# A batch normalisation that streams through two DMA rings: Tile's dependencies in place of hand-made semaphores, and an early 128-byte write by each DMA engine

## The chip, the cores and the metric

One core of a Trainium2 chip. The time is device microseconds of that core. Before: 2484.66 us (median of 3 runs, 2484.28 to 2487.45). With a single core there is no second die to compare; every run listed here except the single one of `touch_allrows` (state unknown) is classed fast.

## The reference

```python
x = np.random.randn(32, 256, 128, 128).astype(np.float32)      # 537 MB
# gamma, beta, running_mean, running_var: 256 floats each
return gamma * (x - mean) / np.sqrt(var + 1e-5) + beta         # per channel
```

Per channel it is one multiply and one add: `scale = gamma / sqrt(var + eps)`, `shift = beta - mean * scale`. All the rest is moving 537 MB in and 537 MB out.

## The kernel before

The input is 64 tiles of 128 rows x 16,384 floats (8.4 MB, 64 KB a row). Three buffers hold tiles. Loads are issued from SyncE and stores from ScalarE: two rings of descriptors on the same 16 DMA engines. Of each tile VectorE does columns 0 to 14,335 in two instructions (2560 columns first), ScalarE the last 2048 (7168 of the last tile). Both rings are paced on purpose: load i waits for the first vector part of tile i-1, and the scalar part of tile i waits until store i-1 has landed.

```python
for i in range(1, NT):                                     # SyncE
    s, turn = i % NBUF, i // NBUF
    if turn:
        nc.sync.wait_ge(stored[s], 16 * turn)              # the buffer is free
    inst = nc.sync.dma_start(out=bufs[s][:], in_=xr[i]).then_inc(loaded[s], 16)
    if turn:
        inst._wait_ge(vdone, 2 * (i - 1) + 1)              # first vector part of tile i-1
# ...
vector_part(0, 0, HW // 2)._wait_ge(early, 16)             # VectorE
vector_part(0, HW // 2, VCOLS)._wait_ge(*landed(0))
for i in range(1, NT):
    vector_part(i, 0, STEP)._wait_ge(*landed(i))           # STEP = 2560
    vector_part(i, STEP, VLAST if i == last else VCOLS)    # VCOLS = 14336
for i in range(last):                                      # ScalarE
    nc.scalar.wait_ge(vdone, 2 * (i + 1))
    inst = scalar_part(i, VCOLS)
    if i:
        inst._wait_ge(stored[(i - 1) % NBUF], 16 * ((i - 1) // NBUF + 1))
    store(i)
```

Of the kernel before, what the change touches and what calls it, by code (L numbers as in the profile page):

```python
# [8 lines left out]
NBUF = 3  # L9


STEP = 2560
VCOLS = 14336
VLAST = 9216


@with_exitstack
def kernel(
    ctx: ExitStack,
    tc: tile.TileContext,  # L20
    x: bass.AP,
    gamma: bass.AP,
    beta: bass.AP,
    running_mean: bass.AP,
    running_var: bass.AP,
    out: bass.AP,
):
    nc = tc.nc
    eps = 1e-5
    f32 = mybir.dt.float32  # L30

    N, C, H, W = x.shape
    P = nc.NUM_PARTITIONS
    assert C % P == 0
    NCB = C // P
    HW = H * W
    NT = N * NCB
    B = 32
    NQ = P // B
    NE = 16  # L40
    NPAR = 4

    xr = x.rearrange("n (cb p) h w -> (n cb) p (h w)", p=P)
    outr = out.rearrange("n (cb p) h w -> (n cb) p (h w)", p=P)

    params = ctx.enter_context(tc.tile_pool(name="params", bufs=1))
    data = ctx.enter_context(tc.tile_pool(name="data", bufs=1))
    bufs = [data.tile([P, HW], f32, name=f"t{s}", tag=f"t{s}") for s in range(NBUF)]
    rows = params.tile([B, NPAR * C], f32, name="rows", tag="rows")
    turned = params.tile([B, NPAR * C], f32, name="turned", tag="turned")  # L50
    par = params.tile([P, NPAR, NCB], f32, name="par", tag="par")
    eps_t = params.tile([P, 1], f32, name="eps_t", tag="eps")
    std_t = params.tile([P, NCB], f32, name="std_t", tag="std")
    rstd_t = params.tile([P, NCB], f32, name="rstd_t", tag="rstd")
    scale_t = params.tile([P, NCB], f32, name="scale_t", tag="scale")
    ms_t = params.tile([P, NCB], f32, name="ms_t", tag="ms")
    shift_t = params.tile([P, NCB], f32, name="shift_t", tag="shift")



    loaded = [tc.alloc_semaphore(f"loaded{s}") for s in range(NBUF)]
    stored = [tc.alloc_semaphore(f"stored{s}") for s in range(NBUF)]
    early = tc.alloc_semaphore("early")
    vdone = tc.alloc_semaphore("vdone")
    adone = tc.alloc_semaphore("adone")
    fetched = tc.alloc_semaphore("fetched")
    vec = tc.alloc_semaphore("vec")
    act = tc.alloc_semaphore("act")

    with tc.tile_critical():  # L70
        count = [0]

        def step(inst, sem=None, value=None):

            if sem is not None:
                inst._wait_ge(sem, value)
            elif count[0]:
                inst._wait_ge(vec, count[0])
            inst.then_inc(vec, 1)
            count[0] += 1  # L80
            return count[0]

        left, right = slice(0, HW // 2), slice(HW // 2, HW)
        last = NT - 1



        nc.sync.dma_start(out=bufs[0][:, left], in_=xr[0][:, left]).then_inc(early, 16)
        zeroed = step(nc.vector.memset(rows[:], 0.0))  # L89
        for r, ap in enumerate((running_var, gamma, beta, running_mean)):  # L90
            inst = nc.sync.dma_start(out=rows[0:NE, r * C : (r + 1) * C], in_=ap.partition_broadcast(NE))  # L91
            if r == 0:
                inst._wait_ge(vec, zeroed)
            inst.then_inc(fetched, 16)
        nc.sync.dma_start(out=bufs[0][:, right], in_=xr[0][:, right]).then_inc(loaded[0], 16)  # L95
        for i in range(1, NT):
            s, turn = i % NBUF, i // NBUF


            if turn:  # L100
                nc.sync.wait_ge(stored[s], 16 * turn)
            inst = nc.sync.dma_start(out=bufs[s][:], in_=xr[i]).then_inc(loaded[s], 16)
            if turn:
                inst._wait_ge(vdone, 2 * (i - 1) + 1)


        step(nc.vector.memset(eps_t[:], eps))  # L107
        step(nc.vector.transpose(out=turned[:], in_=rows[:]), fetched, 16 * NPAR)  # L108

        blocks = turned.rearrange("p (rc q b) -> p rc q b", q=NQ, b=B)  # L110
        flat = par.rearrange("p r cb -> p (r cb)")
        for q in range(NQ):
            placed = step(nc.vector.tensor_copy(out=flat[q * B : (q + 1) * B], in_=blocks[:, :, q, 0]))  # L113
        var_t, gamma_t, beta_t, mean_t = (par[:, r] for r in range(NPAR))
        nc.scalar.activation(  # L115
            out=std_t[:],
            in_=var_t,
            func=mybir.ActivationFunctionType.Sqrt,
            bias=eps_t[:],
            scale=1.0,  # L120
        )._wait_ge(vec, placed).then_inc(act, 1)
        step(nc.vector.reciprocal(out=rstd_t[:], in_=std_t[:]), act, 1)  # L122
        step(nc.vector.tensor_mul(out=scale_t[:], in0=gamma_t, in1=rstd_t[:]))  # L123
        step(nc.vector.tensor_mul(out=ms_t[:], in0=mean_t, in1=scale_t[:]))  # L124
        ready = step(nc.vector.tensor_sub(out=shift_t[:], in0=beta_t, in1=ms_t[:]))  # L125
        nc.vector.wait_ge(vec, ready)

        def vector_part(i, first, end):
            t, cb = bufs[i % NBUF], i % NCB
            return nc.vector.tensor_scalar(  # L130
                out=t[:, first:end],
                in0=t[:, first:end],
                scalar1=scale_t[:, cb : cb + 1],
                scalar2=shift_t[:, cb : cb + 1],
                op0=mybir.AluOpType.mult,
                op1=mybir.AluOpType.add,
            ).then_inc(vdone, 1)

        def scalar_part(i, first):
            t, cb = bufs[i % NBUF], i % NCB  # L140
            return nc.scalar.activation(  # L141
                out=t[:, first:],
                in_=t[:, first:],
                func=mybir.ActivationFunctionType.Identity,
                bias=shift_t[:, cb : cb + 1],
                scale=scale_t[:, cb : cb + 1],
            ).then_inc(adone, 1)

        def landed(i):
            return loaded[i % NBUF], 16 * (i // NBUF + 1)  # L150

        def store(i):
            s = i % NBUF
            nc.scalar.dma_start(out=outr[i], in_=bufs[s][:])._wait_ge(adone, i + 1).then_inc(stored[s], 16)

        vector_part(0, 0, HW // 2)._wait_ge(early, 16)
        vector_part(0, HW // 2, VCOLS)._wait_ge(*landed(0))
        for i in range(1, NT):
            vector_part(i, 0, STEP)._wait_ge(*landed(i))
            vector_part(i, STEP, VLAST if i == last else VCOLS)  # L160
        for i in range(last):
            nc.scalar.wait_ge(vdone, 2 * (i + 1))
            inst = scalar_part(i, VCOLS)
            if i:
                inst._wait_ge(stored[(i - 1) % NBUF], 16 * ((i - 1) // NBUF + 1))
            store(i)
        scalar_part(last, VLAST)._wait_ge(*landed(last))
        nc.scalar.wait_ge(vdone, 2 * NT)
        store(last)

        for s in range(NBUF):
            nc.sync.wait_ge(stored[s], 16 * ((NT - s + NBUF - 1) // NBUF))


# [28 lines left out]
```

## Time and profile before

| | before |
|---|---|
| time, median | 2484.66 us |
| span of the profiled run | 2483.3 us |
| moved | 1073.85 MB, mean 432 GB/s |
| VectorE / ScalarE busy | 20% / 6% |
| a 64 KB DMA packet (median) | 2.418 us |
| store issue after load issue, each turn | 24.6 us |

How the page itself is read stands in the prediction. One measure is used all through and comes from the trace's records of single DMA packets: by how much the 64 KB packets exceed 2.418 us, summed and divided by 16 engines. The part of it at the first store's arrival is called the stretch at the first store, the rest other lengthening.

### The profile page before, as it was taken

Reading aid. Unit: us, or ns where it says so; the run is one execution under the profiler, and the core shown is the slowest. Engines: PE = TensorE matmul, PEld = TensorE weight load, DVE = VectorE, ACT = ScalarE, POOL = GpSimd, SP = SyncE. Lnnn points to the kernel's source line nnn. Section 1 sums busy time; section 2 is a strip of 40 time slices with the busy share of each in tenths; the row PEclk is TensorE's granted clock in tenths of the full one; section 3 lists DMA queues with packets and bytes.
Section 4 is the critical chain, followed back from the end, with each engine's and each line's share of the span. In section 5 each row is a group of like instructions: output and inputs, shape, how many; then the busy total and the mean of one; then the engine's idle time right before and its main releaser. Section 6 shows DMA issues by size and latency. Waiting matters only on the chain.

```text
span 2483.3 us, 516 instructions
## 1 busy us (share of the span) xinstructions
DVE 508.8 (20%) x139; ACT 139.8 (6%) x66; POOL 0.2 (0%) x4
## 2 busy tenths in 40 slices
DVE  3122121221212212122121221212212122121220
ACT  0000000000000000000000000000000000000001
POOL 0000000000000000000000000000000000000000
DMA  9999999999999999999999999999999999999999
GB/s 415 430 439 434 428 436 436 435 433 430 432 433 438 430 432 433 435 424 437 437 428 436 438 436 429 437 435 430 436 437 436 430 437 435 429 437 435 433 433 408
DMA packets 18708, 1073.85 MB, mean 432 GB/s; under 512 B 2128, under 2 KB 2192, under 8 KB 2192
## 3 DMA queue, kind: packets, MB, share of 16 engines
q1 hardware_dynamic: 9488, 536.94, 50.1%
q10 hardware_dynamic: 9216, 536.88, 49.9%
q14 instruction: 4, 0.03, 0.0%
HBM read 536.94 MB, written 536.87 MB: 432 GB/s over the span
## 4 chain that ended last, share of the span: by engine, by line
DMA 93%; DVE 4%; another core or an unknown queue 1%; ACT 0%; issue 0%; SPq 0%; DVEq 0%
DMA t<-in_x_dram 93%; DVE t L130 4%; ACT t L141 0%; SPq L91 0%; DVE rows L89 0%; SPq L95 0%; DVE eps_t L107 0%; DVEq L198 0%; SPq L70 0%
## 5 line engine op out<-in xcount | busy, mean ns | idle before, releaser
L130 DVE TENSOR_SCALAR t<-t,scale_t,shift_t 128x11776 f32<-128x11776 f32 (+2 forms) x128 | 505.3, 3989 | 1930.4 <-DMA t<-in_x_dram 1930.2
L141 ACT ACTIVATE t<-t,shift_t,scale_t 128x2048 f32<-128x2048 f32 x64 | 138.2, 2159 | 2299.3 <-DMA out_dram<-t 2276.6
L108 DVE STREAM_TRANSPOSE turned<-rows 32x1024 f32<-32x1024 f32 x1 | 1.2, 1233 | 12.5 <-DMA rows<-in_running_mean_dram 12.5
L115 ACT ACT_TABLE_LOAD x1 | 1.3, 1283 | 0.9 <-SPq L70 0.9
L89 DVE MEMSET rows<- 32x1024 f32 x1 | 0.9, 912 | 1.2 <-SPq L70 1.2
L115 ACT ACTIVATE std_t<-par,eps_t 128x2 f32<-128x2 f32 x1 | 0.3, 296 | 14.7 <-DVE par L113 14.7
L113 DVE COPY par<-turned 32x8 f32<-32x8 f32 x4 | 0.6, 161 | 0.1
L122 DVE RECIPROCAL rstd_t<-std_t 128x2 f32<-128x2 f32 x1 | 0.2, 166 | 0.4 <-ACT std_t L115 0.4
L125 DVE TENSOR_TENSOR shift_t<-par,ms_t 128x2 f32<-128x2 f32 x1 | 0.2, 161 | 0.0
L124 DVE TENSOR_TENSOR ms_t<-par,scale_t 128x2 f32<-128x2 f32 x1 | 0.2, 161 | 0.0
L123 DVE TENSOR_TENSOR scale_t<-par,rstd_t 128x2 f32<-128x2 f32 x1 | 0.2, 160 | 0.0
L187 POOL MEMSET const-bfloat16-1.0<- 128x1 bf16 x1 | 0.1, 101 | 0.0
L187 POOL MEMSET const-uint8-127<- 128x1 uint8 x1 | 0.1, 101 | 0.0
L187 POOL MEMSET const-float32-0.0<- 128x1 f32 x1 | 0.1, 98 | 0.2 <-issue 0.2
L187 POOL MEMSET const-float32-1.0<- 128x1 f32 x1 | 0.1, 98 | 0.0
L107 DVE MEMSET eps_t<- 128x1 f32 x1 | 0.1, 59 | 0.1
## 6 DMA issues: line engine op xcount, KB each, us to landing
t<-in_x_dram SPq DMA_DIRECT2D x2, 4096.0 KB, 16.5
out_dram<-t ACTq DMA_DIRECT2D x64, 36.5
t<-in_x_dram SPq DMA_DIRECT2D x63, 37.0
rows<-in_running_var_dram SPq DMA_DIRECT2D x1, 16.0 KB, 11.3
rows<-in_gamma_dram SPq DMA_DIRECT2D x1, 16.0 KB, 11.1
rows<-in_beta_dram SPq DMA_DIRECT2D x1, 16.0 KB, 10.9
rows<-in_running_mean_dram SPq DMA_DIRECT2D x1, 16.0 KB, 11.3
```

The lines of the kernel that those rows point to most:

```text
L89: zeroed = step(nc.vector.memset(rows[:], 0.0))
L107: step(nc.vector.memset(eps_t[:], eps))
L108: step(nc.vector.transpose(out=turned[:], in_=rows[:]), fetched, 16 * NPAR)
L113: placed = step(nc.vector.tensor_copy(out=flat[q * B : (q + 1) * B], in_=blocks[:, :, q, 0]))
L115: nc.scalar.activation(out=std_t[:], in_=var_t, func=mybir.ActivationFunctionType.Sqrt, bias=eps_t[:], scale=1.0,)._wait_ge(vec, placed).t ...
L122: step(nc.vector.reciprocal(out=rstd_t[:], in_=std_t[:]), act, 1)
L123: step(nc.vector.tensor_mul(out=scale_t[:], in0=gamma_t, in1=rstd_t[:]))
L124: step(nc.vector.tensor_mul(out=ms_t[:], in0=mean_t, in1=scale_t[:]))
L125: ready = step(nc.vector.tensor_sub(out=shift_t[:], in0=beta_t, in1=ms_t[:]))
L130: return nc.vector.tensor_scalar(out=t[:, first:end], in0=t[:, first:end], scalar1=scale_t[:, cb : cb + 1], scalar2=shift_t[:, cb : cb + 1 ...
L141: return nc.scalar.activation(out=t[:, first:], in_=t[:, first:], func=mybir.ActivationFunctionType.Identity, bias=shift_t[:, cb : cb + 1] ...
L187: nc = _bacc.Bacc("TRN2", target_bir_lowering=False, num_devices=1)
```

## The change

The hand-made semaphores go, and Tile derives the waits from the buffers; two dependencies added by hand keep the pace. New is a touch: before its first store, each DMA engine writes 128 bytes into a row of the first output tile (they are overwritten later), so that whatever a first write costs is paid early.

```diff
-    bufs = [data.tile([P, HW], f32, name=f"t{s}", tag=f"t{s}") for s in range(NBUF)]
-    loaded = [tc.alloc_semaphore(f"loaded{s}") for s in range(NBUF)]
-    # ... seven more kinds of semaphores, and every wait on them
+    data = ctx.enter_context(tc.tile_pool(name="data", bufs=NBUF))
+    ctx.enter_context(tc.manual_schedule())
+    def after(inst, other):
+        info = mybir.DependencyInfo(mybir.DependencyClass.Sync, mybir.DependencyReason.DATA)
+        tc.add_manual_dep(inst.ins, other.ins.name, info, reason="pace of the rings")
 # ...
+    blank = params.tile([P, B], f32, tag="blank")
+    nc.vector.memset(blank[:], 0.0)
+    touch = nc.scalar.dma_start(out=outr[0][0 :: P // NE, 0:B], in_=blank[0 :: P // NE])
 # ...
+        mine = scalar_part(i, VLAST if i == last else VCOLS)
+        if 0 < i < last:
+            after(mine, stores[i - 1])
+        if i == 0:
+            after(mine, touch)
+        stores[i] = nc.scalar.dma_start(out=outr[i], in_=tiles[i][:])
+        if 2 <= i and i + 1 < NT:
+            after(load(i + 1), firsts[i])
```

More of the change, by code (lines that the diff above doesn't have):

```diff
@@ L46 @@
     params = ctx.enter_context(tc.tile_pool(name="params", bufs=1))
-    data = ctx.enter_context(tc.tile_pool(name="data", bufs=1))
-    bufs = [data.tile([P, HW], f32, name=f"t{s}", tag=f"t{s}") for s in range(NBUF)]
-    rows = params.tile([B, NPAR * C], f32, name="rows", tag="rows")
-    turned = params.tile([B, NPAR * C], f32, name="turned", tag="turned")
-    par = params.tile([P, NPAR, NCB], f32, name="par", tag="par")
-    eps_t = params.tile([P, 1], f32, name="eps_t", tag="eps")
-    std_t = params.tile([P, NCB], f32, name="std_t", tag="std")
@@ L54 @@
-    rstd_t = params.tile([P, NCB], f32, name="rstd_t", tag="rstd")
-    scale_t = params.tile([P, NCB], f32, name="scale_t", tag="scale")
-    ms_t = params.tile([P, NCB], f32, name="ms_t", tag="ms")
-    shift_t = params.tile([P, NCB], f32, name="shift_t", tag="shift")
-    loaded = [tc.alloc_semaphore(f"loaded{s}") for s in range(NBUF)]
-    stored = [tc.alloc_semaphore(f"stored{s}") for s in range(NBUF)]
-    early = tc.alloc_semaphore("early")
-    vdone = tc.alloc_semaphore("vdone")
-    adone = tc.alloc_semaphore("adone")
@@ L66 @@
-    fetched = tc.alloc_semaphore("fetched")
-    vec = tc.alloc_semaphore("vec")
-    act = tc.alloc_semaphore("act")
-    with tc.tile_critical():
-        count = [0]
-        def step(inst, sem=None, value=None):
-            if sem is not None:
-                inst._wait_ge(sem, value)
-            elif count[0]:
-                inst._wait_ge(vec, count[0])
-            inst.then_inc(vec, 1)
-            count[0] += 1
-            return count[0]
-        left, right = slice(0, HW // 2), slice(HW // 2, HW)
-        last = NT - 1
-        nc.sync.dma_start(out=bufs[0][:, left], in_=xr[0][:, left]).then_inc(early, 16)
-        zeroed = step(nc.vector.memset(rows[:], 0.0))
-        for r, ap in enumerate((running_var, gamma, beta, running_mean)):
-            inst = nc.sync.dma_start(out=rows[0:NE, r * C : (r + 1) * C], in_=ap.partition_broadcast(NE))
-            if r == 0:
-                inst._wait_ge(vec, zeroed)
-            inst.then_inc(fetched, 16)
-        nc.sync.dma_start(out=bufs[0][:, right], in_=xr[0][:, right]).then_inc(loaded[0], 16)
-        for i in range(1, NT):
-            s, turn = i % NBUF, i // NBUF
-            if turn:
-                nc.sync.wait_ge(stored[s], 16 * turn)
-            inst = nc.sync.dma_start(out=bufs[s][:], in_=xr[i]).then_inc(loaded[s], 16)
-            if turn:
-                inst._wait_ge(vdone, 2 * (i - 1) + 1)
-        step(nc.vector.memset(eps_t[:], eps))
-        step(nc.vector.transpose(out=turned[:], in_=rows[:]), fetched, 16 * NPAR)
-        blocks = turned.rearrange("p (rc q b) -> p rc q b", q=NQ, b=B)
-        flat = par.rearrange("p r cb -> p (r cb)")
-        for q in range(NQ):
-            placed = step(nc.vector.tensor_copy(out=flat[q * B : (q + 1) * B], in_=blocks[:, :, q, 0]))
-        var_t, gamma_t, beta_t, mean_t = (par[:, r] for r in range(NPAR))
-        nc.scalar.activation(
-            out=std_t[:],
-            in_=var_t,
-            func=mybir.ActivationFunctionType.Sqrt,
-            bias=eps_t[:],
-            scale=1.0,
-        )._wait_ge(vec, placed).then_inc(act, 1)
-        step(nc.vector.reciprocal(out=rstd_t[:], in_=std_t[:]), act, 1)
-        step(nc.vector.tensor_mul(out=scale_t[:], in0=gamma_t, in1=rstd_t[:]))
-        step(nc.vector.tensor_mul(out=ms_t[:], in0=mean_t, in1=scale_t[:]))
-        ready = step(nc.vector.tensor_sub(out=shift_t[:], in0=beta_t, in1=ms_t[:]))
-        nc.vector.wait_ge(vec, ready)
-        def vector_part(i, first, end):
-            t, cb = bufs[i % NBUF], i % NCB
-            return nc.vector.tensor_scalar(
-                out=t[:, first:end],
-                in0=t[:, first:end],
-                scalar1=scale_t[:, cb : cb + 1],
-                scalar2=shift_t[:, cb : cb + 1],
-                op0=mybir.AluOpType.mult,
-                op1=mybir.AluOpType.add,
-            ).then_inc(vdone, 1)
-        def scalar_part(i, first):
-            t, cb = bufs[i % NBUF], i % NCB
-            return nc.scalar.activation(
-                out=t[:, first:],
-                in_=t[:, first:],
-                func=mybir.ActivationFunctionType.Identity,
-                bias=shift_t[:, cb : cb + 1],
-                scale=scale_t[:, cb : cb + 1],
-            ).then_inc(adone, 1)
-        def landed(i):
-            return loaded[i % NBUF], 16 * (i // NBUF + 1)
-        def store(i):
-            s = i % NBUF
-            nc.scalar.dma_start(out=outr[i], in_=bufs[s][:])._wait_ge(adone, i + 1).then_inc(stored[s], 16)
-        vector_part(0, 0, HW // 2)._wait_ge(early, 16)
-        vector_part(0, HW // 2, VCOLS)._wait_ge(*landed(0))
-        for i in range(1, NT):
-            vector_part(i, 0, STEP)._wait_ge(*landed(i))
-            vector_part(i, STEP, VLAST if i == last else VCOLS)
-        for i in range(last):
-            nc.scalar.wait_ge(vdone, 2 * (i + 1))
-            inst = scalar_part(i, VCOLS)
-            if i:
-                inst._wait_ge(stored[(i - 1) % NBUF], 16 * ((i - 1) // NBUF + 1))
-            store(i)
-        scalar_part(last, VLAST)._wait_ge(*landed(last))
-        nc.scalar.wait_ge(vdone, 2 * NT)
-        store(last)
-        for s in range(NBUF):
-            nc.sync.wait_ge(stored[s], 16 * ((NT - s + NBUF - 1) // NBUF))
@@ new lines, with load @@
+    data = ctx.enter_context(tc.tile_pool(name="data", bufs=NBUF))
[3 more added lines that the diff above has]
+        tc.add_manual_dep(inst.ins, other.ins.name, info, reason="pace of the rings")
+    last = NT - 1
+    left, right = slice(0, HW // 2), slice(HW // 2, HW)
+    tiles, firsts, stores = {}, {}, {}
+    def load(i):
+        t = data.tile([P, HW], f32, tag="t")
+        tiles[i] = t
+        return nc.sync.dma_start(out=t[:], in_=xr[i])
@@ new lines @@
+    t = data.tile([P, HW], f32, tag="t")
+    tiles[0] = t
+    nc.sync.dma_start(out=t[:, left], in_=xr[0][:, left])
+    rows = params.tile([B, NPAR * C], f32, tag="rows")
+    nc.vector.memset(rows[:], 0.0)
+    for r, ap in enumerate((running_var, gamma, beta, running_mean)):
+        nc.sync.dma_start(out=rows[0:NE, r * C : (r + 1) * C], in_=ap.partition_broadcast(NE))
+    nc.sync.dma_start(out=t[:, right], in_=xr[0][:, right])
+    load(1)
+    load(2)
+    blank = params.tile([P, B], f32, tag="blank")
@@ new lines @@
+    nc.vector.memset(blank[:], 0.0)
+    touch = nc.scalar.dma_start(out=outr[0][0 :: P // NE, 0:B], in_=blank[0 :: P // NE])
+    eps_t = params.tile([P, 1], f32, tag="eps")
+    nc.vector.memset(eps_t[:], eps)
+    turned = params.tile([B, NPAR * C], f32, tag="turned")
+    nc.vector.transpose(out=turned[:], in_=rows[:])
+    par = params.tile([P, NPAR, NCB], f32, tag="par")
+    blocks = turned.rearrange("p (rc q b) -> p rc q b", q=NQ, b=B)
+    flat = par.rearrange("p r cb -> p (r cb)")
+    for q in range(NQ):
+        nc.vector.tensor_copy(out=flat[q * B : (q + 1) * B], in_=blocks[:, :, q, 0])
@@ new lines @@
+    var_t, gamma_t, beta_t, mean_t = (par[:, r] for r in range(NPAR))
+    scale_t = params.tile([P, NCB], f32, tag="scale")
+    shift_t = params.tile([P, NCB], f32, tag="shift")
+    tmp_t = params.tile([P, NCB], f32, tag="tmp")
+    nc.scalar.activation(
+        out=tmp_t[:],
+        in_=var_t,
+        func=mybir.ActivationFunctionType.Sqrt,
+        bias=eps_t[:],
+        scale=1.0,
+    )
+    nc.vector.reciprocal(out=tmp_t[:], in_=tmp_t[:])
+    nc.vector.tensor_mul(out=scale_t[:], in0=gamma_t, in1=tmp_t[:])
@@ new lines, with vector_part, scalar_part @@
+    nc.vector.tensor_mul(out=tmp_t[:], in0=mean_t, in1=scale_t[:])
+    nc.vector.tensor_sub(out=shift_t[:], in0=beta_t, in1=tmp_t[:])
+    def vector_part(i, first, end):
+        t, cb = tiles[i], i % NCB
+        return nc.vector.tensor_scalar(
+            out=t[:, first:end],
+            in0=t[:, first:end],
+            scalar1=scale_t[:, cb : cb + 1],
+            scalar2=shift_t[:, cb : cb + 1],
+            op0=mybir.AluOpType.mult,
+            op1=mybir.AluOpType.add,
+        )
+    def scalar_part(i, first):
+        t, cb = tiles[i], i % NCB
+        return nc.scalar.activation(
+            out=t[:, first:],
+            in_=t[:, first:],
+            func=mybir.ActivationFunctionType.Identity,
+            bias=shift_t[:, cb : cb + 1],
+            scale=scale_t[:, cb : cb + 1],
+        )
@@ new lines @@
+    for i in range(NT):
+        if i == 0:
+            vector_part(0, 0, HW // 2)
+            vector_part(0, HW // 2, VCOLS)
+        else:
+            firsts[i] = vector_part(i, 0, STEP)
+            vector_part(i, STEP, VLAST if i == last else VCOLS)
+        mine = scalar_part(i, VLAST if i == last else VCOLS)
+        if 0 < i < last:
+            after(mine, stores[i - 1])
+        if i == 0:
+            after(mine, touch)
+        stores[i] = nc.scalar.dma_start(out=outr[i], in_=tiles[i][:])
+        if 2 <= i and i + 1 < NT:
+            after(load(i + 1), firsts[i])
```

## The prediction

> **What bounds the kernel now.** I read the page's head and its slices first, then its chain, then its groups of instructions, and last the order of time at both ends of the span.
>
> ```profile
> span 2483.3 us, 516 instructions
> DVE 508.8 (20%) x139; ACT 139.8 (6%) x66; POOL 0.2 (0%) x4
> ...
> DMA  9999999999999999999999999999999999999999
> ...
> GB/s 415 430 439 434 428 436 436 435 433 430 432 433 438 430 432 433 435 424 437 437 428 436 438 436 429 437 435 430 436 437 436 430 437 435 429 437 435 433 433 408
> ...
> DMA t<-in_x_dram 93%; DVE t L130 4%; ACT t L141 0%; SPq L91 0%; DVE rows L89 0%; SPq L95 0%; DVE eps_t L107 0%; DVEq L198 0%; SPq L70 0%
> ...
> L130 DVE TENSOR_SCALAR t<-t,scale_t,shift_t 128x11776 f32<-128x11776 f32 (+2 forms) x128 | 505.3, 3989 | 1930.4 <-DMA t<-in_x_dram 1930.2
> L141 ACT ACTIVATE t<-t,shift_t,scale_t 128x2048 f32<-128x2048 f32 x64 | 138.2, 2159 | 2299.3 <-DMA out_dram<-t 2276.6
> ```
>
> VectorE is busy 20% and ScalarE 6%. The DMA row is 9 in each of the 40 slices. The chain puts 93% on loads, and both compute groups sit idle for a transfer. The kernel is bound by transfer. The chain names loads only because a load and a store are in flight together: a store takes just as many engine packets.
>
> The trace's records of single DMA packets say how full the 16 DMA engines are. A tile is 128 rows of 65,536 bytes, one packet a row, 8 rows an engine. Nearly every such packet took 2.418 us (the median of loads and stores alike). Chaining packets so that each begins where another ended gives 16 unbroken sequences, from about 2.0 us to between 2479.6 and 2481.7 us; the largest gap in any is under 0.2 us. So there is no idle time to win. An engine's bare work is 64 tiles x 8 rows x 2 directions = 1024 packets x 2.418 us = 2476.0 us. What lies above that in the span of 2483.3 us is 7.3 us, 0.3%: about 2.0 us before the first packet, 1.6 us after the last (2483.3 - 2481.7), and the rest lengthened packets. Load packets are longer than 2.418 us by 4.0 us an engine in all (mean of the 16), store packets by 0.05 us.
>
> The part that the change aims at shows in the lengthened ones. All 16 engines have one load packet of 2.74 to 3.64 us that starts between 32.0 and 33.1 us, just as the first store arrives: 0.79 us an engine over 2.418, mean of the 16. At the second store (issued at 76.38 us) nothing like it is recorded. It is a cost of the first store alone.
>
> ```profile
> 0.90 1.28 ACT L115 ACT_TABLE_LOAD   x1 [0.90 <-SPq L70]
> 0.95 0.38 SPq L88 DMA_DIRECT2D t<-in_x_dram  x1
> ...
> 23.85 3.48 DVE L130 TENSOR_SCALAR t<-t,scale_t,shift_t 128x6144 f32<-128x6144 f32 x1 [1.27 <-DMA t<-in_x_dram]
> 27.36 2.09 ACT L141 ACTIVATE t<-t,shift_t,scale_t 128x2048 f32<-128x2048 f32 x1 [10.23 <-DVE t L130]
> 29.49 0.37 ACTq L154 DMA_DIRECT2D out_dram<-t  x1
> ...
> 76.38 0.34 ACTq L154 DMA_DIRECT2D out_dram<-t  x1
> ```
>
> Columns are start, duration, engine and line. The first store goes out at 29.49 us, and some 2 us later every engine's load packet is stretched.
>
> **What the Trainium skill says.** "DMA: Bandwidth & Descriptors", section "Where 436 GB/s comes from", gives 435.2 GB/s as the ceiling of the 16 ports. The trace agrees: 16 x 65,536 bytes / 2.418 us = 433.7 GB/s, and the page's mean is 432. Its section "Issuing engines are not separate DMA queues" says that transfers started by different engines share the same 16 DMA engines and interleave; the records agree, load and store packets alternating on one engine where both rings have work. So no new order of issue can beat the packet sum. Its section "Specifications" asks for at least 512 bytes for line rate, below which there is a read-modify-write; the touch writes 128 bytes. The trace has no 128-byte packet; its nearest, the parameters' 1024-byte packets, took about 0.05 us.
>
> **The change, part by part.**
>
> 1. *Hand-made semaphores become Tile's dependencies.* The order on the two rings stays. Load i+1 waited for store i-2 (its buffer) and for the first vector part of tile i; it still does, by the pool's three slots and by the added dependency. The scalar part of tile i waited for store i-1; it still does. New waits can come from Tile's own bookkeeping, a few tens of ns of queue time each (the trace has 0.02 to 0.05 us between a release and the next instruction). After a load lands, the ring is without a load for about 3.6 us (1.62 us of vector part, then 2 us from issue to packet), which the store covers: the sequences have no gap. So some 0.1 us more in each of 61 turns costs 0, not 6 us, as long as the other ring has packets. Steady state: 0 us.
>
> 2. *Tile 0.* The scalar part waited for both vector parts (idle 10.23 us, released by DVE at 27.36 us). In the new code it depends on its own columns' load, scale and shift, and the touch. If Tile tells columns apart it starts near 23.9 us, and the first store goes out when the vector part ends, about 27.4 us, 2.1 us earlier. If Tile takes the tile as a whole, the first vector part waits for both halves: 23.85 + 4.55 + 3.48 + 2.09 = 34.0 us, 4.5 us later. Loads 1 and 2 are queued until long after, so the engines have work in either case: 0 us, except for the tail (rival 2).
>
> 3. *The touch.* One memset of 128x32, about 0.06 us by the eps_t row (59 ns), and one issue on ScalarE's queue of about 0.34 us, both in time that these engines spend waiting. On the DMA side each engine writes one packet of 128 bytes: 0.05 us by the 1024-byte packets, at most about 0.2 us with a read-modify-write (a guess). Added: 0.1 us.
>
> 4. *What the touch takes away.* At best the whole 0.79 us. Whether it does depends on whether the first write's stall is hidden. Issued near 2.3 us, the touch reaches the engines about 1 us later (the first load: issued at 0.95, first packet at 1.95 us), when their first load packets are still running and are themselves slow (1.57 to 2.45 us where later 32,768-byte ones took 1.213: 0.65 us over, mean of 16). Two slow starts at one time can overlap. Or the stall only moves from 32 us to 4 us and holds up a load packet there. I take half: -0.4 us.
>
> 5. *Ends.* The same two dependencies rule the start of the first load and the last store. Tile's closing waits on each transfer semaphore may add a few waits of 0.05 us after the last packet: +0.1 us or so, inside the noise.
>
> Sum: 0 + 0 + 0.1 - 0.4 + 0.1 = -0.2 us. 2484.66 - 0.2 = 2484.4; three runs of before lie at 2484.28, 2484.66 and 2487.45, and I take **2484.3 us**.
>
> **The rivals.**
>
> *1. The touch wins all of it, or the stall is only moved.* For the first: no later store stalls, so something is paid once. Against: the touch runs beside the first loads, on engines that are never idle, and what is paid once must be paid somewhere. All won: 2484.66 - 0.8 + 0.1 = 2484.0 us. Only moved: 2484.66 + 0.1 = 2484.8, up to 2485.5 if the small write costs more than I take.
>
> *2. The tail opens a gap.* The end of the span in order of time:
>
> ```profile
> 2435.87 0.34 ACTq L154 DMA_DIRECT2D out_dram<-t  x1
> 2448.30 6.36 ACT L141 ACTIVATE t<-t,shift_t,scale_t 128x7168 f32<-128x7168 f32 x1 [12.46 <-DMA t<-in_x_dram]
> 2448.30 5.27 DVE L130 TENSOR_SCALAR t<-t,scale_t,shift_t 128x2560 f32<-128x2560 f32 x2 [30.70 <-DMA t<-in_x_dram]
> 2454.70 0.34 ACTq L154 DMA_DIRECT2D out_dram<-t  x1
> ```
>
> The last store is issued at 2454.70 and can reach the engines near 2456.7 us. By the packet records the last but one store keeps them busy until 2460.3 to 2462.4 us, so there are 3.6 to 5.7 us in hand. A first store 2.1 us earlier goes in one packet slot (2.4 us) sooner and shifts the two rings against each other for the whole run, the last load landing up to 2.4 us later. That leaves 1.2 us. A shift of two packets would leave a gap of about 1.2 us: 2485.6 us. A later first store only adds to what is in hand.
>
> *3. Tile adds a wait that binds.* If a load came to wait for the store just before it (a shared semaphore, or the whole output taken as one region), one ring would run dry in each turn. The store's landing in the trace falls about 15 us before the next load's landing, so a load held to the store after it would cost several us a turn: 61 x 4 us = 244 us, 2730 us. Against: with three slots, the store waited for is two tiles old, and the dependencies added by hand repeat the old ones exactly. I give it 1%.
>
> **Range and chances.** The best case is 2484.0 us, the gap in the tail 2485.6. Lengthened loads add noise: groups of them near 598, 947, 1063 and 1140 us make most of the 3.2 us an engine that the first store does not explain, and they seem to fall at random; before's runs spread over 3.2 us. So 2482.0 to 2487.5 should hold it 8 times in 10. Faster by 2% would need 2435 us, below the bare packet sum of 2476.0: no order can do it. Slower by 2% needs about 2534 us, that is rival 3.
>
> **What would show each step.** Right: packets still of 2.418 us and unbroken sequences; loads still waiting for the first vector part and an older store; no stretched packets at the first large store. For step 4, packets near 3 to 5 us should be no longer than before if the stall is hidden, and about 0.8 us longer if it was moved. Step 2 shows in the start of the first scalar part, 23.9, 27.4 or 32 us. Wrong: a large idle of the loads' queue on the newest store, gaps above 0.5 us in the packet sequences, or packets over 2.42 us in steady state.

## More of the kernel before

One turn late in the run (start, duration, engine and line; the first line merges two loads), 2397.27 - 2372.68 = 24.6 us:

```profile
2372.68 38.95 SPq L102 DMA_DIRECT2D t<-in_x_dram  x2
...
2397.27 0.34 ACTq L154 DMA_DIRECT2D out_dram<-t  x1
```

The load ring's queue waited in the kernel before for an old store and for the first vector part, 61 times each (us in total, times, longest):

```profile
SPq L101 <- DMA out_dram<-t: 1398.1, 61, 68.8
SPq L102 <- DVE t L130: 985.0, 61, 16.2
```

## The result, and the profile after

2486.04 us (median of 6 runs, 2484.0 to 2487.36); before, in the same rounds, 2485.11 us (6 runs, 2484.28 to 2487.45). The ratio is 1.0003, 95% interval 0.999 to 1.0015: the same. Ratios here are the mean time of one kernel's fast runs over that of the other's of the same rounds, so not quite the ratio of the medians quoted.

The page of the changed kernel, in the lines that answer those of before:

```profile
span 2485.3 us, 760 instructions
DVE 508.8 (20%) x140; ACT 139.8 (6%) x66; POOL 0.2 (0%) x4
...
DMA  9999999999999999999999999999999999999999
...
DMA t<-in_x_dram 91%; DVE t L112 4%; ACT t L123 0%; DVEq L112 0%; SPq L72 0%; SPq L62 0%; DVE rows L70 0%; DVE blank L80 0%; DVE eps_t L85 0%
...
L123 ACT ACTIVATE t<-t,shift_t,scale_t 128x2048 f32<-128x2048 f32 x64 | 138.2, 2159 | 2304.7 <-DMA out_dram<-t 2280.7
```

The page grew from 516 to 760 instructions, while busy time and the instructions counted as busy stayed (one memset more): the added ones are waits on semaphores (146 semaphore instructions before, 397 after). The DMA row is still full. Next, the order of time at the start of the changed kernel (start, duration, engine and line):

```profile
1.98 0.59 ACTq L81 DMA_DIRECT2D out_dram<-blank  x1
2.60 1.28 ACT L98 ACT_TABLE_LOAD   x1 [2.60 <-DVE eps_t L85]
...
23.15 3.48 DVE L112 TENSOR_SCALAR t<-t,scale_t,shift_t 128x6144 f32<-128x6144 f32 x1 [1.33 <-DMA t<-in_x_dram]
23.24 2.09 ACT L123 ACTIVATE t<-t,shift_t,scale_t 128x2048 f32<-128x2048 f32 x1 [6.78 <-DMA t<-in_x_dram]
26.71 0.36 ACTq L145 DMA_DIRECT2D out_dram<-t  x1
```

Tile tells columns apart: the scalar part of tile 0 runs beside the vector part, and the first store goes out at 26.71 in place of 29.49 us. Then the end, in order of time:

```profile
2416.26 0.33 SPq L62 DMA_DIRECT2D t<-in_x_dram  x1
...
2435.83 0.34 ACTq L145 DMA_DIRECT2D out_dram<-t  x1
2453.04 6.36 ACT L123 ACTIVATE t<-t,shift_t,scale_t 128x7168 f32<-128x7168 f32 x1 [17.24 <-DMA t<-in_x_dram]
2453.14 5.27 DVE L112 TENSOR_SCALAR t<-t,scale_t,shift_t 128x2560 f32<-128x2560 f32 x2 [30.64 <-DMA t<-in_x_dram]
2459.43 0.34 ACTq L145 DMA_DIRECT2D out_dram<-t  x1
```

The last but one store is issued as before (2435.83), but the last load lands 4.7 us later (2453.04 against 2448.30). About half of that is this run's greater length. Counted back from the end of the last packet of the run, the last load's packets end at 33.8 us in place of 36.2: one packet slot (2.4 us) later. The early first store put the store ring one packet ahead and the load ring one packet behind for the whole run, so the phase of the two rings (the issue of a store less that of the load before it) fell by two, from 24.6 us to 19.7 us. (All nine profiles of section 6 show this pair: 36.2 us at the longer phase, 33.8 us at the shorter.) Last, what the load ring's queue waited for (us in total, times, longest):

```profile
SPq L62 <- DVE t L112: 1804.3, 61, 38.5
SPq L62 <- DMA out_dram<-t: 575.8, 31, 60.4
...
SPq L62 <- DMA out_dram<-blank: 4.3, 1, 4.3
```

All 61 paced loads end their wait on the first vector part, as meant. One wait is new: load 2 waits 4.3 us for the touch. The trace shows one completion semaphore for both, so the second can't be issued until the first has landed. The touch is not the reason as such: eight completion semaphores serve all transfers by turns, and load 2 gets the one that the touch has. Without the touch (`after_notouch`) it gets that of tile 0's first load and goes out later still, at 13.1 us. Here load 2 goes out at 9.13 us, long before the engines need it: load 1 lands at 55 us.

The two profiled spans differ by 2.0 us (2483.3 and 2485.3). In the packet records, other lengthening is 3.3 us before and 5.8 us after; the stretch at the first store is 0.79 and 0.55 us. Span less both is 2479.2 and 2479.0 us. So the whole difference lies in lengthened load packets. Does the kernel cause them, or chance?

### The profile page after: what moved, and what is told of

It is laid out like the page before. It is cut to its first block, busy times and chain, and to the rows that moved or that the text cites. A ratio compares the mean times of both kernels' runs of the same rounds, so it can differ in the third digit from the quotient of the medians.

```text
span 2485.3 us, 760 instructions
## 1 busy us (share of the span) xinstructions
DVE 508.8 (20%) x140; ACT 139.8 (6%) x66; POOL 0.2 (0%) x4
## 4 chain that ended last, share of the span: by engine, by line
DMA 91%; DVE 4%; another core or an unknown queue 2%; issue 0%; ACT 0%; DVEq 0%; SPq 0%
DMA t<-in_x_dram 91%; DVE t L112 4%; ACT t L123 0%; DVEq L112 0%; SPq L72 0%; SPq L62 0%; DVE rows L70 0%; DVE blank L80 0%; DVE eps_t L85 0%
```

## The experiments

Twelve kernels. Two theories at first: the change moves well under 1 us and the rest is chance, or its parts (touch, phase) act on the length of packets.

### 1. Each kernel a second time

No edit but a comment. The changed kernel (`after_again`):

> The changed kernel, unaltered, for a second profile. It tells what of the +2.0 us between the two profiled spans (2483.3 and 2485.3 us) belongs to the kernel. Theory 1 (the change moves under 1 us, the rest is load packets lengthened at random): ratio to before between 0.9995 and 1.0010; the stretch at the first store stays near 0.55 us an engine and the first store's packets near 32.4 us, but the other lengthening of load packets, 5.8 us an engine in the first profile of it, comes out anywhere from 2.5 to 6.5 us. Theory 2 (the new phase of the two rings lengthens reads): it comes out at 5 us or more again, and the ratio is 1.0005 or more.

The kernel before (`before_again`):

> The kernel before, unaltered, for a second profile and as the zero of this call. Both theories: ratio 1.000 within 0.0006, stretch at the first store near 0.79 us an engine. Theory 1: the other lengthening of load packets, 3.3 us an engine in the first profile, moves by 1 us or more. Theory 2: it stays between 2.8 and 3.8 us.

Measured: the changed kernel 2483.7 us, ratio 0.9996 (0.9984 to 1.0009); before 2482.28 us, ratio to itself 0.9994 (0.9981 to 1.0006). Other lengthening fell from 5.8 to 2.0 us for the changed kernel and from 3.3 to 0.6 us for the one before. (Theory 1 had given 2.5 to 6.5 us for the changed kernel; 2.0 is below even that.) It is not a fixed property of a kernel; it varies from run to run by as much as the difference to be explained. The stretch at the first store came out at 0.86 us for the changed kernel (0.55 expected) and 0.40 us for the one before (0.79 expected): that varies just as much, and in the wrong direction for the touch. My expectation of both stretches was wrong.

### 2. Each part alone

The changed kernel without the touch (`after_notouch`):

```diff
-    blank = params.tile([P, B], f32, tag="blank")
-    nc.vector.memset(blank[:], 0.0)
-    touch = nc.scalar.dma_start(out=outr[0][0 :: P // NE, 0:B], in_=blank[0 :: P // NE])
 # ...
-        if i == 0:
-            after(mine, touch)
```

> The changed kernel without the touch and what waits for it: Tile's dependencies alone. If the touch is what took the stretch at the first store from 0.79 to 0.55 us an engine, the stretch is back at 0.75 to 0.85 us. If it fell because the first store now goes out 2.8 us earlier, it stays near 0.55 us. Time: both say within 1 us of the changed kernel, ratio to before 0.9995 to 1.0010.

Measured: 2484.82 us, ratio 1.0002 (0.9989 to 1.0014), stretch 0.68 us.

The kernel before with the touch (`before_touch`):

```diff
+    touched = tc.alloc_semaphore("touched")
 # ...
+        blanked = step(nc.vector.memset(blank[:], 0.0))
+        nc.scalar.dma_start(out=outr[0][0 :: P // NE, 0:B], in_=blank[0 :: P // NE])._wait_ge(vec, blanked).then_inc(touched, 16)
 # ...
+        nc.scalar.wait_ge(touched, 16)
         for i in range(last):
```

> The kernel before with the touch alone, by hand-made semaphores. If the touch shortens the stretch, it is 0.5 to 0.6 us an engine here, and 0.75 to 0.85 us if it was the earlier first store. Time: 0.2 us less than before at best, so ratio 0.9993 to 1.0007; nothing that the time alone can show.

Measured: 2483.76 us, ratio 0.9997 (0.9983 to 1.001), stretch 0.57 us. Neither part moves the time by more than the interval, 0.2% at most. The two stretches lie inside the spread that identical kernels show (0.40 to 0.86), so they say nothing.

### 3. A touch of all 128 rows

```diff
-    touch = nc.scalar.dma_start(out=outr[0][0 :: P // NE, 0:B], in_=blank[0 :: P // NE])
+    touch = nc.scalar.dma_start(out=outr[0][:, 0:B], in_=blank[:])
```

> The touch on all 128 rows of the first output tile, 128 bytes each, 8 packets an engine, so every address page that the first store begins to write has been written. If what is paid at the first store goes with the address of the rows, the stretch falls to under 0.2 us an engine. If it goes with the first load of full store traffic and not with any first address, it stays between 0.4 and 0.9 us, the spread of the six profiles so far (0.40 to 0.86). Time the same.

Measured (one run): 2485.99 us, stretch 0.70 us. Having written to each row of the tile beforehand does not remove the stretch. So it is not a cost of the first access to the start of those rows; the rest of each 64 KB row was not touched, and a cost that goes with it is not excluded.

### 4. How much wait the rings bear

My prediction put Tile's extra waits at zero because the other ring covers them. A large wait should show whether that reason holds. In `late_load` each load waits for the second vector part:

```diff
-            firsts[i] = vector_part(i, 0, STEP)
-            vector_part(i, STEP, VLAST if i == last else VCOLS)
+            vector_part(i, 0, STEP)
+            firsts[i] = vector_part(i, STEP, VLAST if i == last else VCOLS)
```

> In the changed kernel each load waits for the second vector part in place of the first: 6.4 us later in each of 61 turns (the second part took 6.41 us). My theory: the 16 DMA engines have packets of the other ring meanwhile (load ring empty some 10 us of a turn of 38.7 us, store ring some 4.5 us, not at the same time), so the turns cost nothing: within 5 us of the changed kernel, a packet sequence without gaps over 0.3 us until the end, at most one gap of 1 to 5 us before the last store, whose load lands later. Rival (a delay in the chain of loads costs its length, since the chain puts over 90% on loads): 61 x 6.4 = 390 us more, some 2875 us.

Measured: 3726.56 us, ratio 1.5007 (1.4982 to 1.5032). Both theories failed, mine by 1240 us, and the rival too by 850. The order of time of this run, one turn (the first line merges four loads):

```profile
442.29 179.59 SPq L62 DMA_DIRECT2D t<-in_x_dram  x4
442.31 0.35 ACTq L145 DMA_DIRECT2D out_dram<-t  x1
493.77 7.93 DVE L112 TENSOR_SCALAR t<-t,scale_t,shift_t 128x2560 f32<-128x2560 f32 x2 [51.55 <-DMA t<-in_x_dram]
493.83 2.10 ACT L123 ACTIVATE t<-t,shift_t,scale_t 128x2048 f32<-128x2048 f32 x1 [57.38 <-DMA out_dram<-t]
501.80 0.35 ACTq L145 DMA_DIRECT2D out_dram<-t  x1
```

The load and the store are issued 0.02 us apart, and they land together too (what waits for them starts at 493.77 and 493.83 us). The same turn cut into stretches (us, busy of each engine, clock, DMA share, GB/s):

```profile
442.30:490.00 47.70, 0.00 (x0) 0.00 (x0) 0.00 (x0) 1.00 0.94 350
490.00:502.00 12.00, 7.93 (x2) 2.10 (x1) 0.00 (x0) 1.00 0.01 5
```

The rings have fallen into step. There is nothing to move while VectorE works, and when both run they move 350 GB/s, although the DMA engines are busy for 94% of that stretch. In the packet records an engine is idle for 848 us of the run (ends included; the kernel before has 5 us by this count), and the 64 KB packets are 396 us longer (load packets 3.04 us on average, stores 2.58). Why packets get longer when both rings restart together was not found. The phase was 6.6 us at the third store and 0.0 from the fourth on.

That suggested a new theory: in each turn either ring is empty for a while, from the landing to the next first packet. The load ring's emptiness contains the first vector part (1.61 us), the store ring's the scalar part (2.09 us). If the load ring's is longer, the store ring gets more packets in a turn and gains on it, until a store has to wait for the tile that has just landed. Two values of `STEP` tested it, with all else as in the changed kernel:

```diff
-STEP = 2560
+STEP = 4096        # and 6144 in the second run
```

> The changed kernel with a first vector part of 4096 columns: each load waits for it some 0.96 us longer (1.61 us x 4096/2560 = 2.58 us). New theory from the late loads: the time from a landing to the next first packet is then longer on the load ring than on the store ring (first part 2.58 us against the scalar part's 2.09 us), so the store ring gains on the load ring, at most 0.5 us a turn; packets come whole (2.418 us), and so small a difference may be held, as the kernel before holds the opposite one (1.62 against 2.09 us, phase of store to load 24.6 us all along). Held: phase constant, 2480 to 2490 us. Not held: the phase falls turn by turn until both rings restart together, packets lengthen, and the run is 5 to 50% slower.

> The changed kernel with a first vector part of 6144 columns: 1.61 x 6144/2560 = 3.87 us, 2.25 us longer than now and 1.8 us over the scalar part. New theory: over half a packet a turn cannot be held, the store ring catches up with the load ring within some 15 to 30 turns, both then restart together as in the run with the late loads, and the time lies between 2600 and 3700 us. Rival (only the time without packets counts, which is covered): within 5 us of the changed kernel.

Measured: `step_4096` 2488.69 us, ratio 1.0025 (1.0012 to 1.0039), phase 18.9 us from the fourth store to the last. It has no gap either: its 64 KB packets are 7.2 us an engine longer than 2.418 us each, more than in any of the nine profiles of section 6 (1.0 to 6.3), and its span less that is 2478.4 us. `step_6144` 2646.72 us, ratio 1.0658 (1.0644 to 1.0673); the phase falls 15.5, 10.6, 6.2, 4.5 us over four turns and stays at 4.5. One late turn of it, in order of time:

```profile
2075.71 7.94 DVE L112 TENSOR_SCALAR t<-t,scale_t,shift_t 128x6144 f32<-128x6144 f32 x2 [33.36 <-DMA t<-in_x_dram]
2079.26 0.33 SPq L62 DMA_DIRECT2D t<-in_x_dram  x1
2080.42 2.09 ACT L123 ACTIVATE t<-t,shift_t,scale_t 128x2048 f32<-128x2048 f32 x1 [39.18 <-DMA out_dram<-t]
2083.73 0.34 ACTq L145 DMA_DIRECT2D out_dram<-t  x1
```

The store no longer follows its scalar part (which ended at 2082.51) but the vector part (2075.71 + 7.94 = 2083.65): the store ring has caught up and waits for data. An engine is now idle for 61 us, and packets are 106 us longer. Both outcomes agree with the theory: a load ring 0.5 us behind was held, one 1.8 us behind was not. Two values do not locate the limit. The drift took four turns where I had expected 15 to 30. That whole packets hold the phase for small differences fits, but was not tested by itself.

### 5. A wait for the newest store, and no pace at all

Two slots instead of three (`two_bufs`), which is the wait that rival 3 feared:

```diff
-NBUF = 3
+NBUF = 2
 # ...
-    load(2)
 # ...
-        if 2 <= i and i + 1 < NT:
+        if 1 <= i and i + 1 < NT:
```

> The changed kernel with two slots in place of three, so that each load waits for the newest store: the wait that rival 3 of the prediction feared. Theory: load and store of a turn then both start behind the same landing, both rings run dry together, and each of some 62 turns has about 2 us (the time from issue to packet) without packets: gaps of 1.5 to 3 us a turn, about 2610 us (2570 to 2680). If the rings were still covered, 2485 us.

Measured: 2733.77 us, ratio 1.1002 (1.098 to 1.1024). The time lies above the expected 2570 to 2680 us. The idle time came out as expected (136 us an engine, 2.2 us in each of 62 turns, or 2.1 without the 5 us at the ends). What I had not expected is that packets lengthen by another 120 us, nearly all in the first five packet slots after a load's issue.

Without the two dependencies added by hand (`unpaced`):

```diff
-        if 0 < i < last:
-            after(mine, stores[i - 1])
 # ...
-            after(load(i + 1), firsts[i])
+            load(i + 1)
```

> The changed kernel without the two dependencies added by hand (a load on the first vector part, a scalar part on the last store): only buffers and data order the rings. Theory (the engines are full and any order that keeps them full takes the packet sum): the same time within 5 us, span less lengthened packets 2478 to 2480 us, or some us more where the last store waits. Rival (the pace itself keeps reads from being lengthened): lengthening of load packets above 7 us an engine and more than 1% slower.

Measured: 2511.63 us, ratio 1.011 (1.0095 to 1.0125). Lengthened packets come to 24 us an engine, and after 2477 us some engines have gaps of 8 to 16 us before the last store, as far as packets can be assigned to engines (the records carry no engine number). The pace is worth 1.1%, split between tidy packets and a full tail. My theory (within 5 us) failed. Both numbers of the rival were met: load packets were 10.9 us longer (above 7), and the run was more than 1% slower. It named only a part of the loss, though: store packets were longer too, by 13.1 us, and the gaps in the tail come to some 13 us an engine.

### 6. The phase by itself

`after_latestore`, the changed kernel with the first store sent out as late as before:

```diff
-            vector_part(0, HW // 2, VCOLS)
+            half = vector_part(0, HW // 2, VCOLS)
 # ...
             after(mine, touch)
+            after(mine, half)
```

> The changed kernel with one dependency more: tile 0's scalar part waits for tile 0's vector part, as in the kernel before. The first store should be issued near 28.8 us and the phase of store to load be 24.6 us again in place of 19.7. If the phase is what raised the lengthening of load packets (mean 2.0 us an engine in three profiles at 24.6, 4.1 us in four at 19.7), it is 0.5 to 3.5 us here and the ratio to before about 0.9997; if that difference is chance, it may be anywhere from 0.5 to 6 us, and the ratio is 0.9990 to 1.0010 either way.

`before_early`, the kernel before with the first store sent out as early as in the changed one:

```diff
+        nc.scalar.wait_ge(vec, ready)
         for i in range(last):
-            nc.scalar.wait_ge(vdone, 2 * (i + 1))
+            if i:
+                nc.scalar.wait_ge(vdone, 2 * (i + 1))
             inst = scalar_part(i, VCOLS)
 # ...
+            else:
+                inst._wait_ge(*landed(0))
+                nc.scalar.wait_ge(vdone, 2)
```

> The kernel before, with tile 0's scalar part waiting for its own columns' load instead of the vector parts, which sends the first store out near 27.4 us: the phase of store to load should become 19.7 us with the hand-made semaphores kept. If the phase raises the lengthening, it is 2.5 to 6 us an engine and the ratio to before 1.0003 to 1.0012. If not, 0.5 to 6 us with no pattern, and the ratio is 1.000 within 0.0006.

Measured: the phases moved as meant (24.5 and 19.8 us). Times 2484.0 and 2483.84 us, both with ratio 1.0005 (0.9991 to 1.0018, and 0.9992 to 1.0017). The nine profiles of this family together, us an engine:

| run | touch | phase | stretch at first store | other lengthening | span | span less both |
|---|---|---|---|---|---|---|
| before | no | 24.6 | 0.79 | 3.29 | 2483.3 | 2479.2 |
| before_again | no | 24.6 | 0.40 | 0.64 | 2480.3 | 2479.3 |
| before_touch | yes | 24.6 | 0.57 | 2.16 | 2482.0 | 2479.3 |
| after_latestore | yes | 24.5 | 0.48 | 0.56 | 2480.2 | 2479.2 |
| before_early | no | 19.8 | 0.42 | 1.02 | 2480.6 | 2479.2 |
| after | yes | 19.7 | 0.55 | 5.77 | 2485.3 | 2479.0 |
| after_again | yes | 19.7 | 0.86 | 1.98 | 2481.7 | 2478.9 |
| after_notouch | no | 19.7 | 0.68 | 4.28 | 2483.6 | 2478.6 |
| touch_allrows | all rows | 19.7 | 0.70 | 4.47 | 2483.9 | 2478.7 |

The last column is constant within 0.7 us: but for that, the spans differ by lengthened packets alone. `after_latestore` and `before_early` ran on chip 1, the others of known chip on chip 11, so the two of them compare the phases; the table as a whole does not. Other lengthening averages 1.7 us in the four runs at 24.6 and 3.5 us in the five at 19.7, but the sets overlap (0.56 to 3.29 against 1.02 to 5.77), and sending the first store out early (`before_early`) did not raise it to the 2.5 to 6 us of the theory that the phase does it. Whether the phase matters at this level stays open: the means differ by 1.8 us, and the interval of `before_early` allows up to 0.17%, or 4 us.

In all these runs the lengthened load packets sit where one of the two rings has just restarted: in the first profile of before 1.7 of the 3.3 us fall 4.8 to 7.3 us after a load's issue and 0.9 us 2.4 to 4.8 us after a store's. The stretch at the first store sits at such a place too: in that profile 2.5 to 3.6 us after the store's issue. So it may be the same effect, there on all 16 engines at once, where the longest later group (near 1063.5 us, just after a load's restart) has six packets of 3.3 to 3.6 us. No run tests this. What decides how long packets get in a given run was not found.

## Why the prediction was right or wrong

The verdict (the same) was right. The time was predicted as 2484.3 us and came out at 2486.04, inside the range, and the changed kernel's second set of runs gave 2483.7. What carried the verdict is the bound. The sum of -0.2 us over the five steps is too small for the times to test (the interval of the ratio, 0.999 to 1.0015, is -2.5 to +3.7 us), so that it falls near the result says nothing for its terms, and steps 4 and 5 were wrong. By the steps:

- **The bound** held. The packets are still of 2.418 us, the sequences still unbroken up to the last store, and the bare packet sum left nothing to win. Two readings around it were off. The budget above the sum does not close: 2.0 + 1.6 + 4.05 us of packets is 7.7, where 7.3 was to be explained. And the four groups of long load packets, near 598, 947, 1063 and 1140 us, hold 1.3 us of the 3.2, not most of it; nor do they fall at random, but where a ring has just restarted (section 6).
- **Step 1, dependencies: 0 us.** Right for what Tile adds: the ratio without the touch is 1.0002 (0.9989 to 1.0014). But after a load lands its ring stays empty for longer than the 3.6 us given: 1.6 us of vector part and, in the trace of before, 3.85 us (median) from a load's issue to its first packet. And its reason was too broad. A wait is free "as long as the other ring has packets" only while the two rings keep their phase. Another 0.96 us a turn cost 0.25%, 2.25 us cost 6.6%, 6.4 us cost 50%.
- **Step 2, tile 0.** Right: the scalar part at 23.24 us, the first store at 26.71 (23.9 and 27.4 predicted).
- **Step 3, the cost of the touch: 0.1 us.** Right in kind and too large: the 16 packets took 0.013 us each, and the load packets beside them kept their 1.213 us. The touch's packets came at 6.06 to 7.58 us, later than the 3 to 5 us given.
- **Step 4, what it takes away: -0.4 us.** This failed. I took one measured stretch, 0.79 us, for a fixed cost. It ranges from 0.40 to 0.86 us; the mean is 0.63 us in the five runs with a touch and 0.57 in the four without. There is no gain to see, and nothing was moved to the time of the touch either. The touch, at 128 bytes, does not take the stretch away. Nor was "a cost of the first store alone" shown: other load packets lengthen where a ring restarts.
- **Step 5, ends: +0.1 us.** The sign was wrong. Tile's program starts its first packet at 1.74 us (1.95 before) and ends 1.3 us after the last packet (1.6 before).
- **Rival 2, the tail.** Its working was right: the last load came one packet slot later against the end of the run, for which it left 1.2 us in hand, and 1.1 us was left. The last store, issued at 2459.43 us, could by the prediction's 2 us reach the engines near 2461.4, and its packets began at 2462.57, directly behind the one before. The 2 us are too long: in the four runs whose engines stood idle before the last store (`late_load`, `step_6144`, `two_bufs`, `unpaced`) its first packet came 0.84 us after the issue, so some 2.3 us were in hand.
- **Rival 3, a wait that binds,** did not come. Tile does let transfers share a semaphore, as the rival feared, but with eight in turn the other one is eight transfers, or four turns, old. Put in on purpose (`two_bufs`), it gave 2734 us where the rival said 2730. That agreement is partly luck: it had 4 us of empty rings a turn; measured were 2.2 us, and as much again in lengthened packets.

No version tried beats the kernel before: the parts and the phase come out within 0.1% of it (intervals within 0.2%), and every other variant that was timed in rounds is slower.

## What to carry to other kernels

When the DMA engines have no gap from the first packet to the last, look at the packet sum first: here it said at once that re-writing the synchronisation could win at most the 7.3 us (0.3%) above it. Two rings that share the engines have a phase. Here it was set by when the first store went out, and it held while the compute between a landing and the next issue took the load ring at most 0.5 us longer than the store ring (`step_4096`); at 1.8 us longer it fell. Keep the load ring's part no longer than the store ring's: in the runs where they restarted together (`late_load`) or nearly so (`step_6144`) the engines ran dry and packets lengthened. A cost below the run-to-run spread must be profiled more than once before anyone builds a remedy for it.

## What the Trainium skill lacked or had wrong

- "DMA: Bandwidth & Descriptors", "Rules for kernel authors", says that spreading DMAs over SP and ACT gives no bandwidth, since they share the engines. It lacks that their timing can take bandwidth away: loads and stores issued 0.02 us apart ran at 350 GB/s with the engines busy 94% of the stretch and load packets of 3.04 us, where the same transfers 19.7 or 24.6 us apart ran at 432 GB/s with packets of 2.418 us.
- The same page, "Queues, rings and completion order", describes packets of some 9 to 17 descriptors before an engine changes rings. The trace's records, chained by their times, alternate load and store after each single 64 KB row where both rings have work, in a tile of which each engine has 8 rows.
- The same page's 512-byte minimum for line rate ("Specifications") comes without the size of the cost. Here it agrees as to rate: 128 bytes in 0.013 us are 9.8 GB/s an engine, where 64 KB in 2.418 us are 27.1. But one such packet an engine cost nothing that shows.
- No page has the stretch of load packets when a run's first large store arrives (0.40 to 0.86 us an engine in nine profiles), nor the lengthening of load packets where a ring restarts (0.6 to 5.8 us an engine over a whole run, changing from run to run of one kernel).
